# Two of four weight block sums of a Strassen product made by accumulating DMAs

## The chip, the cores and the metric

The kernel runs on one core of one Trainium2 chip. The metric is the device time of one execution in microseconds; before and after the change it is the median of several runs.

## The reference

One layer of a hybrid diffusion backbone is computed for 128 context tokens and 512 latent tokens (640 in all, width 1024) with shared weights in float32:

```
u = RMSNorm(h) * (1 + scale1) + shift1
z = u @ w_in                       # 1024 x 6656, split into q, k, v, B, C, x_in, g_att, g_conv
A = GQA attention(q, k, v) @ w_att_out
Bm = (B * dwconv3(C * x_in)) @ w_conv_out
h = h + gate1 * RMSNorm((sigmoid(g_att) * A + sigmoid(g_conv) * Bm) @ w_o)
h = h + gate2 * RMSNorm(conv_ffn(RMSNorm(h) * (1 + scale2) + shift2))
```

The change touches the product `u @ w_in` for the columns of g_att, C, x_in, B and g_conv.

## The kernel before

Every float32 operand of a product is split into a high part (a cast to float32r on ScalarE, `hi_of`, L1174) and a low part (the rest, a subtraction on VectorE, `lo_of`, L1178). A product is then three matmuls: high x high, high x low and low x high. Right operands (the tokens' side) are kept in that form for the whole stage; weights come through the sync engine (SP) into a pool of three rooms `raw` of 128 x 1024 and are split on the way.

The columns of `w_in` named above are worked through in 19 pairs of blocks of 128 columns (`PAIRS`: three for g_att, then C, X, B for each of four indices, then four for g_conv). Each pair is one step of Strassen's algorithm in Winograd's form: the weights of a pair are four blocks, each 512 deep and 128 wide. They are a11 and a12, the upper and the lower half in depth of the first column block, and a21 and a22 of the second one. Seven products of 12 matmuls (128 x 128 x 320) are made instead of eight, in the order A11, A12, S2, S1, S3, S4, A22. `PLACE` says in which part and half the left operand of each lies. Four of them are sums of blocks, kept in `MS`, four parts of 512 columns in `WB`: M1 = a21 + a22 (step S1), M2 = M1 + a11 (S2), M3 = a11 + a21 (S3) and M4 = M2 + a12 (S4). They are all additions; the signs are in the right operands and in the results.

`mix(m)` issues pair m. TensorE, ScalarE and VectorE run in the order in which the code is written (`manual_schedule`); between two steps stand the copies out of PSUM (`copied`, `added`), the splits for later steps (`mhi` for ScalarE's half, `lo_of` for VectorE's), the sums of the next pair (`msums`, three groups of additions at L1282), and extra work that comes with the results of the pair before (`more`: gates, convolution taps, shift sums `shift_add` in `XG`). Part 0 of the left operands is a11 and a12, part 1 is M1 and M2, part 2 is M3 and M4, part 3 is a22.

The sync engine's and GpSimd's queues are ordered by a scheduler in this stage; each of them runs its entries in turn, and an entry that waits holds the later ones. `mload(n)` loads a whole column block (512 KB) into the next room of the pool: `mix` calls it for the two blocks of the pair after next. After the last pair the same function loads `w_conv_out` in blocks for the next stage. Outside the stage GpSimd does attention work (L879) and norms; within it, it has nothing.

Of the kernel before, what the change touches and what calls it, by code (L numbers as in the profile page):

```python
# [14 lines left out]
ALU = mybir.AluOpType  # L15
# [3 lines left out]
KT = 8  # L19
# [44 lines left out]
def trunk_layer(ctx, tc, x_prompt, x_sample, cache_k, cache_v, c, c_ctx, w_ada, b_ada, g_pre1, g_post1, g_pre2,  # L64
                g_post2, w_in, q_norm, k_norm, w_att_out, conv_w, w_conv_out, w_o, w_up, conv_ffn, w_down, rope,
                y_prompt, y_sample, new_k, new_v):
    nc = tc.nc
    V, S, G, PE = nc.vector, nc.scalar, nc.gpsimd, nc.tensor

    w_ada, b_ada, w_in, w_o, w_up, w_down = w_ada[0], b_ada[0], w_in[0], w_o[0], w_up[0], w_down[0]  # L70
    w_att_out, w_conv_out, conv_w, conv_ffn = w_att_out[0], w_conv_out[0], conv_w[0], conv_ffn[0]
# [22 lines left out]
    def nm(s):  # L94
        cnt[0] += 1
        return f"{s}_{cnt[0]}"
# [19 lines left out]
    def ps2():  # L116
        return ps.tile([128, 1024], F32, tag="s2", name=nm("s2"), bufs=3)

    def ps1():
        return psa.tile([128, 512], F32, tag="s1", name=nm("s1"), bufs=2)  # L120
# [9 lines left out]
    def raw_tile():  # L130
        return wp.tile([128, 1024], F32, tag="raw", name=nm("raw"), bufs=3)
# [192 lines left out]
    with tc.tile_pool(name="pro", bufs=2) as pro, tc.manual_schedule(engines={mybir.EngineType.SP}):  # L324
# [237 lines left out]
        for f in range(2, KT):  # L562
# [5 lines left out]
            if f == 2:  # L568
# [11 lines left out]
                both = [kvp_.tile([128, 9, HD], F32, name=x) for x in ("tabq", "tabk")]  # L580
# [24 lines left out]
            if f == KT - 2:  # L605
                cut_upto(9)
                p = ps1()
# [16 lines left out]
    with tc.tile_pool(name="att", bufs=2) as at:  # L624
# [329 lines left out]
        p = ps2()[:, 0:512]  # L954
# [205 lines left out]
    def bank(i):  # L1160
        if i >= 2 and len(pools) == 1:
            early.close()
            pools.append(ctx.enter_context(tc.tile_pool(name="pb", bufs=1, space=bass.MemoryType.PSUM)))
        return pools[i >= 2].tile([128, 512], F32, tag=f"b{i}", name=nm(f"b{i}"))


    cut, raws, pair, TT = {}, {}, {}, {}

    def hi_of(key, raw, to=None):
        n = raw.shape[1]  # L1170
        if to is None:
            to = tuple(wp.tile([128, 1024], F32R, tag=x, name=nm(x), bufs=3)[:, :n] for x in ("whi", "wlo"))
        cut[key] = (raw, *to)
        S.activation(to[0], raw, AF.Copy)  # L1174

    def lo_of(key):
        raw, hi, lo = cut[key]
        V.tensor_tensor(out=lo, in0=raw, in1=hi.bitcast(F32), op=ALU.subtract)  # L1178

    def block(out, key, half, right, start, stop):  # L1180
        _, hi, lo = cut[key]
        wh, wl = (y[:, half * 512:half * 512 + 512] for y in (hi, lo))
        th, tl = TT[right]
        for k in range(4):
            ws = slice(k * 128, (k + 1) * 128)
            for n, (p, q) in enumerate(((wh, th), (wh, tl), (wl, th))):
                PE.matmul(out, p[:, ws], q[:, k, :], start=start and k == 0 and n == 0, stop=stop and k == 3 and n == 2,  # L1187
                          skip_group_check=True)
# [28 lines left out]
    MS = WB[:, 2 * NTOK:2 * NTOK + 2048]  # L1217
# [37 lines left out]
    PAIRS = [("GA", i) for i in range(1, 4)] + [(x, i) for i in range(4) for x in "CXB"] + [("GC", i) for i in range(4)]  # L1255
    NP = len(PAIRS)
    AT = {"GA": O_GA, "C": O_C, "X": O_X, "B": O_B, "GC": O_GC}
    ROWS_OF = {"C": 0, "X": 1, "B": 2}

    def mrows(m):  # L1260
        x, i = PAIRS[m]
        r = ROWS_OF[x] if x in ROWS_OF else (i - 1 if x == "GA" else i)
        return ROWS[2 * r], ROWS[2 * r + 1]

    def col_load(key, w, c0):
        raw = raws[key] = raw_tile()
        nc.sync.dma_start(raw.rearrange("p (k c) -> p k c", c=128), w[:, c0:c0 + 128].rearrange("(k p) c -> p k c", p=128))

    def mload(n):

        if n < 2 * NP:
            x, i = PAIRS[n // 2]
            col_load(("m", n // 2, n % 2), w_in, AT[x] + (2 * i + n % 2) * 128)
        elif n < 2 * NP + KT:
            col_load(("v", n - 2 * NP), w_conv_out, (n - 2 * NP) * 128)

    def msums(m):
        a1, a2 = raws["m", m, 0], raws["m", m, 1]
        s1, s2, s3, s4 = (MS[:, i * 512:(i + 1) * 512] for i in range(4))

        def add(out, a, b):
            V.tensor_tensor(out=out, in0=a, in1=b, op=ALU.add)  # L1282

        def both():
            add(s1, a2[:, 0:512], a2[:, 512:1024])
            add(s3, a1[:, 0:512], a2[:, 0:512])
        return both, lambda: add(s2, s1, a1[:, 0:512]), lambda: add(s4, s2, a1[:, 512:1024])

    def mhi(m, part):
        src = {0: raws["m", m, 0], 1: MS[:, 0:1024], 2: MS[:, 1024:2048], 3: raws["m", m, 1][:, 512:1024]}[part]  # L1290
        hi_of(("m", m, part), src)

    def vcut(j):
# [3 lines left out]
    def mix(m, extra):  # L1297

        d0, d1 = mrows(m)
        nxt = m + 1 if m + 1 < NP else None  # L1300
        pair["m", m] = tuple(bank((3 * m + i) % 8)[:, 0:HT] for i in range(3))

        def step(x):
            b = 1 if x == "A12" else 2 if x in ("S1", "S4") else 0
            part, half = PLACE[x]
            block(pair["m", m][b], ("m", m, part), half, "m" + RIGHT[x], x in ("A11", "A12", "S1"), True)

        def more(i):
            for f in extra.get(i, ()):
                f()  # L1310

        if m:
            mix_last(m - 1)
        lo_of(("m", m, 1))
        more(0)
        step("A11")

        copied(("m", m), "p1", 0, HT)
        more(1)
        step("A12")  # L1320

        mhi(m, 2)
        added(d0[:, 0:HT], ("m", m), "p1", 1)
        lo_of(("m", m, 2))
        more(2)
        step("S2")

        copied(("m", m), "u2", 0, HT)
        more(3)
        step("S1")  # L1330

        copied(("m", m), "p5", 2, HT)
        mhi(m, 3)
        adds = msums(nxt) if nxt else None
        if nxt:
            adds[0]()
        more(4)
        step("S3")

        added(d1[:, HT:], ("m", m), "p5", 0)  # L1340
        lo_of(("m", m, 3))
        mload(2 * m + 4)
        if nxt:
            mhi(nxt, 0)
            lo_of(("m", nxt, 0))
            adds[1]()
        else:
            vcut(0)
        more(5)
        step("S4")  # L1350

        if nxt:
            mhi(nxt, 1)
        added(d0[:, HT:], ("m", m), "u2", 2)
        if nxt:
            adds[2]()
        mload(2 * m + 5)
        more(6)
        step("A22")

    def mix_last(m):
        S.activation(mrows(m)[1][:, 0:HT], pair["m", m][0], AF.Copy)
# [8 lines left out]
    for j in range(KT):  # L1371
        unit = next_unit()
        if j == 6:
            for n in range(3):
                mload(n)
        if j < 6:
            for f in making[2 * j:2 * j + 2]:
                f()
        elif j == 7:
            adds = msums(0)  # L1380
            adds[0]()
            mhi(0, 0)
            lo_of(("m", 0, 0))
            adds[1]()
            mhi(0, 1)
            adds[2]()
            mload(3)
        outs = plain_gemm(j, *unit.parts, AH, AL)
        for out, (b0, b1) in zip(outs, BLKS):
            if j < 2:  # L1390
                times(MA[:, j, b0:b1], out, MA[:, KT - 2 + j, b0:b1])
            else:
                S.activation(MA[:, j, b0:b1], out, AF.Copy)
# [53 lines left out]
    for m, (x, i) in enumerate(PAIRS):  # L1447
# [18 lines left out]
        elif before[0] == "X":  # L1466
            c0, c1, y0, y1 = ROWS[:4]
# [7 lines left out]
        elif before[0] == "B":  # L1475
            c0, c1, y0, y1, b0, b1 = ROWS[:6]
# [28 lines left out]
    for j in range(KT):  # L1505
        if j + 1 < KT:
            vcut(j + 1)
        else:
            cut_upto(state["next"] + 1)
        if 0 < j < KT - 3:  # L1510
            mload(2 * NP + j + 3)
        elif j:
            fetch(state["next"] + min(j - 4, 2))
        if j == 0:
            gate_load(graws[0], 2, 0)
        if j < KT - 1:
            gate_load(graws[j + 1], 2, j + 1)
        if j == 5:
            gate_vectors(gvec, 2, g_post1)
        _, hi, lo = cut["v", j]  # L1520
        outs = plain_gemm(j + 2, hi, lo, BH, BL)
        sg = ROWS[j]
        for h, (out, (b0, b1)) in enumerate(zip(outs, BLKS)):
            times(sg[:, b0:b1], out, sg[:, b0:b1])
            if h == 0 and j:
                gate_add(gaccs, graws[j], j, 0)
        V.tensor_tensor(out=sg, in0=sg, in1=MA[:, j, :], op=ALU.add)
        for row in range(0 if j == 0 else 1, 2):
            gate_add(gaccs, graws[j], j, row)
        mh, ml = MH[j // 4][:, j % 4, :], ML[j // 4][:, j % 4, :]  # L1530
        S.activation(mh, sg, AF.Copy)
        minus(ml, sg, mh.bitcast(F32))
# [389 lines left out]
    for q in range(4):  # L1922
# [7 lines left out]
        elif q == 1:  # L1930
            half_load(0)
            p = bank(6)
# [114 lines left out]
    adds = right_sums(0, HALF)  # L2047
# [18 lines left out]
    adds = sums(2)  # L2066
# [103 lines left out]
    w, x, y = NJ - 3, NJ - 2, NJ - 1  # L2170
# [96 lines left out]
```

## Time and profile before

| what | us |
|---|---|
| median of 3 runs | 1110.13 (1109.88 to 1110.19) |
| span of the profiled execution | 1108.4 |
| stage of the 19 pairs, about | 320 to 555 |
| TensorE busy in the span | 1098.6 |
| VectorE busy | 843.6 |
| ScalarE busy | 577.2 |
| GpSimd busy | 145.4 |

The span runs from the first to the last instruction of the profiled execution; it is 1.7 us below the median of the runs, and the profile states no other time for that execution. In the profile's lines, PE is TensorE's matmul, PEld its weight load (which overlaps PE), DVE is VectorE, ACT ScalarE, POOL GpSimd, SPq the queue of the sync engine. A line `L1282 DVE ... x18 | 12.3, 686 | 1.1 <-DMA raw` reads: line of the code, engine, operation, tiles, count, busy microseconds in total, mean nanoseconds of one, idle microseconds just before, and what ended them. In an order of time the first number is the start, the second the length.

### The profile page before, as it was taken

How to read it: one execution, taken by the hardware profiler on the slowest of the kernel's cores; microseconds unless marked ns; L12 is line 12 of the kernel's file. 1: busy time of each engine (PE TensorE's matmuls, PEld its weight loads, DVE VectorE, ACT ScalarE, POOL GpSimd, SP SyncE). 2: the span in 40 equal slices, each digit the busy share in tenths (PEclk: the TensorE clock that was granted, in tenths of full speed). 3: DMA queues.
4: the chain of work that ended last, by engine and by line, in shares of the span. 5: the costliest groups of instructions: out<-in, count | busy, mean ns of one | idle time of the engine just before them, and what ended most of it. 6: DMA issues, size and time to landing. Idle time of an engine off the chain costs nothing.

```text
span 1108.4 us, 19227 instructions
## 1 busy us (share of the span) xinstructions
PE 1098.6 (99%) x7633; PEld 1012.9 (91%) x7633; DVE 843.6 (76%) x1352; ACT 577.2 (52%) x1021; POOL 145.4 (13%) x190
## 2 busy tenths in 40 slices
PE   8999999999999999999999999999999999999998
PEld 6798888889999999999999789999999999998886
DVE  5687766755559889988678558898899889989544
ACT  5486776764335444455422356655565545546442
POOL 1067666651000000000000021000000000000001
PEclk9999999999999999999999999999999999999999
DMA  9832102102224323332254655234344333435722
GB/s 318 246 101 79 58 25 73 39 4 73 76 78 130 108 79 99 108 89 77 81 188 151 212 170 153 77 101 126 112 133 132 106 114 119 127 101 184 261 93 95
DMA packets 157415, 130.07 MB, mean 117 GB/s; under 512 B 6410, under 2 KB 135942, under 8 KB 157326
## 3 DMA queue, kind: packets, MB, share of 16 engines
q1 hardware_dynamic: 157214, 128.81, 37.9%
q8 instruction: 60, 0.98, 0.4%
q14 instruction: 29, 0.24, 0.1%
q10 hardware_dynamic: 112, 0.04, 0.0%
HBM read 117.39 MB, written 11.44 MB: 116 GB/s over the span
## 4 chain that ended last, share of the span: by engine, by line
PE 97%; DMA 2%; ACT 1%; DVE 0%; issue 0%; DVEq 0%; SPq 0%; ACTq 0%
PE b L1187 46%; PE b L183 10%; PE b L185 10%; PE b L184 9%; PE s L704 3%; PE s L892 3%; PE s L183 3%; PE s L916 3%; PE s L185 3%; PE s L184 3%; DMA raw<-in_w_in_dram 1%; DMA araw<-in_w_ada_dram 1%; PE b L1786 1%; PE s L675 0%; PE s L238 0%; DMA XT<-in_x_sample_dram 0%
## 5 line engine op out<-in xcount | busy, mean ns | idle before, releaser
L1187 PE MATMUL b<-ZBr,whi 128*128 128x320 f32 x688 | 152.1, 309 | 0.0
L1187 PE MATMUL b<-MT,whi 128*128 128x320 f32 x608 | 134.2, 309 | 0.0
L1187 PEld LDWEIGHTS b<-ZBr,whi 128*128 128x128 f32 x688 | 115.0, 188 | 0.1
L1187 PE MATMUL b<-ZBr,wlo 128*128 128x320 f32 x344 | 106.2, 309 | 0.0
L1187 PEld LDWEIGHTS b<-MT,whi 128*128 128x128 f32 x608 | 101.6, 188 | 0.0
L1187 PE MATMUL b<-MT,wlo 128*128 128x320 f32 x304 | 94.1, 309 | 0.0
L879 POOL TENSOR_TENSOR pr<-pr,sm 128x640 f32<-128x640 f32 x64 | 80.0, 1260 | 53.7 <-DVE sm L878 47.4
L1174 ACT ACTIVATE whi<-SUM 128x1024 fp32r<-128x1024 f32 x40 | 42.2, 1055 | 78.5 <-DVE SUM L1701 76.0
L1731 DVE SCALAR_TENSOR_TENSOR Y<-C,cffn,Y 128x642 f32<-128x642 f32 x88 | 77.6, 882 | 0.9
L149 DVE TENSOR_TENSOR wlo<-raw,whi 128x1024 fp32r<-128x1024 f32 (+1 forms) x32 | 35.4, 1106 | 54.9 <-ACT whi L148 54.6
L869 ACT ACTIVATE pr<-s,mx,rq 128x640 f32<-128x640 f32 x64 | 56.6, 885 | 32.5 <-DVE mx L856 29.1
L1187 PE MATMUL b<-ZBT,whi 128*128 128x320 f32 x320 | 71.1, 309 | 0.0
L1187 PE MATMUL b<-UL,whi 128*128 128x320 f32 x228 | 70.8, 311 | 0.0
L1187 PE MATMUL b<-UH,wlo 128*128 128x320 f32 x228 | 70.1, 307 | 0.0
L1187 PE MATMUL b<-UH,whi 128*128 128x320 f32 x228 | 69.7, 306 | 0.0
L1174 ACT ACTIVATE whi<-WB 128x1024 fp32r<-128x1024 f32 x38 | 40.1, 1055 | 55.8 <-DVE WB L1282 55.8
L1178 DVE TENSOR_TENSOR wlo<-raw,whi 128x1024 fp32r<-128x1024 f32 (+1 forms) x51 | 50.4, 1018 | 20.1 <-ACT whi L1174 20.1
L1187 PEld LDWEIGHTS b<-ZBr,wlo 128*128 128x128 f32 x344 | 64.6, 188 | 0.0
L183 PE MATMUL s<-whi,UH 128*128 128x256 f32 (+1 forms) x197 | 64.4, 327 | 0.0
L851 DVE TENSOR_REDUCE mx<-s 128x1 f32<-128x640 f32 x64 | 52.5, 820 | 14.0 <-PE s L704 13.5
L1195 ACT ACTIVATE p<-b 128x320 f32<-128x320 f32 x78 | 34.1, 438 | 55.3 <-PE b L1187 53.5
L185 PE MATMUL s<-whi,UL 128*128 128x256 f32 (+1 forms) x197 | 59.9, 304 | 0.0
(401 smaller groups left out, 3191.7 us busy)
## 6 DMA issues: line engine op xcount, KB each, us to landing
raw<-in_w_in_dram SPq DMA_DIRECT2D x48, 512.0 KB
RAW<-in_w_up_dram SPq DMA_DIRECT2D x40, 512.0 KB
raw<-in_w_down_dram SPq DMA_DIRECT2D x22, 512.0 KB
raw<-in_w_ada_dram SPq DMA_DIRECT2D x16, 512.0 KB
actd<-Y SPq DMA_DIRECT2D x18, 321.0 KB
XT<-in_w_ada_dram SPq DMA_DIRECT2D x9, 512.0 KB
raw<-in_w_att_out_dram SPq DMA_DIRECT2D x8, 512.0 KB
raw<-in_w_conv_out_dram SPq DMA_DIRECT2D x8, 512.0 KB
```

The source lines that it names most:

```text
L149: V.tensor_tensor(out=lo[:, :n], in0=raw, in1=hi[:, :n].bitcast(F32), op=ALU.subtract)
L183: PE.matmul(out, ah, bh, start=start, stop=False)
L184: PE.matmul(out, ah, bl, start=False, stop=False)
L185: PE.matmul(out, al, bh, start=False, stop=stop)
L851: V.tensor_reduce(out=mx, in_=self.sc[h], axis=AX.X, op=ALU.max, negate=True)
L869: S.activation(pr, self.sc[h], AF.Exp, bias=mx, scale=rs, accum_out=sm)
L879: G.tensor_tensor(out=pr, in0=pr, in1=sm.broadcast_to((128, NTOK)), op=ALU.mult)
L1174: S.activation(to[0], raw, AF.Copy)
L1178: V.tensor_tensor(out=lo, in0=raw, in1=hi.bitcast(F32), op=ALU.subtract)
L1187: PE.matmul(out, p[:, ws], q[:, k, :], start=start and k == 0 and n == 0, stop=stop and k == 3 and n == 2, skip_group_check=True)
L1195: S.activation(t, pair[j][b], AF.Copy)
L1731: V.scalar_tensor_tensor(out=y, in0=crows(j)[i][:, d:d + NACT], scalar=cffn[:, 44 * d + o:44 * d + o + 1], in1=y, op0=ALU.mult, op1=ALU.add)
```

## The change

Of each pair's blocks, the two sums M1 and M3 are no longer added by VectorE. The sync engine loads block a21 into the place of the sum, once for M1 and once for M3, and GpSimd issues a transfer from SBUF to SBUF that adds a22 (for M1) or a11 (for M3) to what lies there. The first column block (a11 and a12) has two rooms in turn, a22 two halves of a third room; these three rooms of the pool stay with the stage for its length. VectorE keeps the two other additions, M2 and M4. The loads are issued at other points of `mix`: into M1 after its low part has been made, into M3 likewise, a1 (a11 and a12) of the pair after next before step S3, a22 after it.

```diff
--- before.py
+++ after.py
@@ -1266,28 +1266,43 @@
         raw = raws[key] = raw_tile()
         nc.sync.dma_start(raw.rearrange("p (k c) -> p k c", c=128), w[:, c0:c0 + 128].rearrange("(k p) c -> p k c", p=128))
 
-    def mload(n):
-
-        if n < 2 * NP:
-            x, i = PAIRS[n // 2]
-            col_load(("m", n // 2, n % 2), w_in, AT[x] + (2 * i + n % 2) * 128)
-        elif n < 2 * NP + KT:
-            col_load(("v", n - 2 * NP), w_conv_out, (n - 2 * NP) * 128)
+    M1, M2, M3, M4 = (MS[:, i * 512:(i + 1) * 512] for i in range(4))
+    mrooms = {}
+
+    def mrooms_open():
+        a, b, c = (raw_tile() for _ in range(3))
+        mrooms["a1"], mrooms["a22"] = (a, b), (c[:, 0:512], c[:, 512:1024])
+
+    def mload(m, what):
+
+        if m >= NP:
+            j = 2 * (m - NP) + (what == "a22")
+            if what in ("a1", "a22") and j < KT:
+                col_load(("v", j), w_conv_out, j * 128)
+            return
+        x, i = PAIRS[m]
+        row, k, nk = {"a1": (0, 0, 8), "a22": (1, 4, 4), "s1": (1, 0, 4), "s3": (1, 0, 4)}[what]
+        if what in mrooms:
+            dst = raws["m", m, what] = mrooms[what][m % 2]
+        else:
+            dst = {"s1": M1, "s3": M3}[what]
+        c0 = AT[x] + (2 * i + row) * 128
+        nc.sync.dma_start(dst.rearrange("p (k c) -> p k c", c=128),
+                          w_in[k * 128:(k + nk) * 128, c0:c0 + 128].rearrange("(k p) c -> p k c", p=128))
+        if what == "s1":
+            G.dma_start(dst, raws["m", m, "a22"], accum_op=ALU.add)
+        elif what == "s3":
+            G.dma_start(dst, raws["m", m, "a1"][:, 0:512], accum_op=ALU.add)
 
     def msums(m):
-        a1, a2 = raws["m", m, 0], raws["m", m, 1]
-        s1, s2, s3, s4 = (MS[:, i * 512:(i + 1) * 512] for i in range(4))
+        a1 = raws["m", m, "a1"]
 
         def add(out, a, b):
             V.tensor_tensor(out=out, in0=a, in1=b, op=ALU.add)
-
-        def both():
-            add(s1, a2[:, 0:512], a2[:, 512:1024])
-            add(s3, a1[:, 0:512], a2[:, 0:512])
-        return both, lambda: add(s2, s1, a1[:, 0:512]), lambda: add(s4, s2, a1[:, 512:1024])
+        return lambda: add(M2, M1, a1[:, 0:512]), lambda: add(M4, M2, a1[:, 512:1024])
 
     def mhi(m, part):
-        src = {0: raws["m", m, 0], 1: MS[:, 0:1024], 2: MS[:, 1024:2048], 3: raws["m", m, 1][:, 512:1024]}[part]
+        src = {0: raws.get(("m", m, "a1")), 1: MS[:, 0:1024], 2: MS[:, 1024:2048], 3: raws["m", m, "a22"]}[part]
         hi_of(("m", m, part), src)
 
     def vcut(j):
@@ -1312,6 +1327,8 @@
         if m:
             mix_last(m - 1)
         lo_of(("m", m, 1))
+        if nxt:
+            mload(nxt, "s1")
         more(0)
         step("A11")
 
@@ -1322,6 +1339,8 @@
         mhi(m, 2)
         added(d0[:, 0:HT], ("m", m), "p1", 1)
         lo_of(("m", m, 2))
+        if nxt:
+            mload(nxt, "s3")
         more(2)
         step("S2")
 
@@ -1332,18 +1351,17 @@
         copied(("m", m), "p5", 2, HT)
         mhi(m, 3)
         adds = msums(nxt) if nxt else None
-        if nxt:
-            adds[0]()
+        mload(m + 2, "a1")
         more(4)
         step("S3")
 
         added(d1[:, HT:], ("m", m), "p5", 0)
         lo_of(("m", m, 3))
-        mload(2 * m + 4)
+        mload(m + 2, "a22")
         if nxt:
             mhi(nxt, 0)
             lo_of(("m", nxt, 0))
-            adds[1]()
+            adds[0]()
         else:
             vcut(0)
         more(5)
@@ -1353,8 +1371,7 @@
             mhi(nxt, 1)
         added(d0[:, HT:], ("m", m), "u2", 2)
         if nxt:
-            adds[2]()
-        mload(2 * m + 5)
+            adds[1]()
         more(6)
         step("A22")
 
@@ -1371,20 +1388,19 @@
     for j in range(KT):
         unit = next_unit()
         if j == 6:
-            for n in range(3):
-                mload(n)
+            mrooms_open()
+            for m, what in ((0, "a1"), (0, "a22"), (0, "s1"), (0, "s3"), (1, "a1"), (1, "a22")):
+                mload(m, what)
         if j < 6:
             for f in making[2 * j:2 * j + 2]:
                 f()
         elif j == 7:
             adds = msums(0)
-            adds[0]()
             mhi(0, 0)
             lo_of(("m", 0, 0))
+            adds[0]()
+            mhi(0, 1)
             adds[1]()
-            mhi(0, 1)
-            adds[2]()
-            mload(3)
         outs = plain_gemm(j, *unit.parts, AH, AL)
         for out, (b0, b1) in zip(outs, BLKS):
             if j < 2:
@@ -1508,7 +1524,7 @@
         else:
             cut_upto(state["next"] + 1)
         if 0 < j < KT - 3:
-            mload(2 * NP + j + 3)
+            mload(NP + (j + 3) // 2, ("a1", "a22")[(j + 3) % 2])
         elif j:
             fetch(state["next"] + min(j - 4, 2))
         if j == 0:
```

## The prediction

> **What bounds the kernel now.** I read the page first, then the windows of the stage that the change touches (the 19 pairs of column blocks, 320 to 555 us), TensorE's waits in it, the groups of instructions by shape, and last the order of time on VectorE for single pairs.
>
> ```profile
> span 1108.4 us, 19227 instructions
> ...
> PE 1098.6 (99%) x7633; PEld 1012.9 (91%) x7633; DVE 843.6 (76%) x1352; ACT 577.2 (52%) x1021; POOL 145.4 (13%) x190
> ...
> L879 POOL TENSOR_TENSOR pr<-pr,sm 128x640 f32<-128x640 f32 x64 | 80.0, 1260 | 53.7 <-DVE sm L878 47.4
> ```
> ```profile
> core 0: us, PE busy (x) PEld busy (x) DVE busy (x) ACT busy (x) POOL busy (x), PEclk, DMA share, GB/s
> 320.00:555.00 235.00, 235.00 (x1611) 233.78 (x1610) 196.90 (x283) 115.50 (x181) 0.00 (x0) 1.00 0.34 97
> ```
> ```profile
> PEld b L1187 <- issue: 0.6, 1, 0.6
> PEld b L1441 <- issue: 0.2, 1, 0.2
> PEld b L301 <- issue: 0.2, 1, 0.2
> PEld b L1187 <- DVE wlo L1178: 0.2, 1, 0.2
> ```
>
> TensorE sets the end: 99% busy over the whole span, busy all through the stage at a granted clock of 1.00. All the gaps before its weight loads in the stage add up to 1.2 us, and only 0.2 us of them ended with VectorE. VectorE is busy 196.9 of 235 us there, GpSimd not at all, and the DMA engines 34%. So work that is taken off VectorE has almost nothing to give back; what matters is whether the new route delivers in time.
>
> ```profile
> 320.18 135.05 PE b L1187 x924
> ```
>
> 924 matmuls are 11 pairs of 84, so a pair takes 12.28 us and a step (12 matmuls) 1.75 us. Pair m starts at 320.18 + 12.28 m; its third step, S2, 3.5 us later.
>
> **What is removed.** Per pair two additions on VectorE go: a21+a22 (S1's block, M1) and a11+a21 (S3's block, M3).
>
> ```profile
> L1282 DVE TENSOR_TENSOR WB<-raw 128x512 f32<-128x512 f32 x18 | 12.3, 686 | 1.1 <-DMA raw<-in_w_in_dram 0.9
> L1282 DVE TENSOR_TENSOR WB<-raw,raw 128x512 f32<-128x512 f32 x18 | 12.3, 684 | 0.0
> ```
>
> That is 12.3 + 12.3 = 24.6 us of VectorE in this window. All of it lies beside matmuls, so it is worth at most the 0.2 us that TensorE waited for VectorE, and nothing more.
>
> **What is added, and how it is chained.** For each pair the sync engine now loads a21 twice, into M1 and into M3 (256 KB each), and GpSimd adds a22 and a11 to these with an accumulating transfer of 256 KB, which must wait until the plain load has landed. In the order in which the changed kernel issues its transfers, the queue of the sync engine runs per pair: a1 of the pair after next, s1 (into M1), s3 (into M3), a22. GpSimd's queue holds only the two accumulations in turn. Two of the waits are new and tie these queues into one chain: a1 goes into a room from which the last s3 accumulation still reads, so it waits for that to land; and s1, which stands behind a1 in the queue, waits with it. VectorE then waits for M1 before its first remaining addition, with everything behind it (the other addition, the copies out of PSUM, the low part for S1 and S2).
>
> Where VectorE frees M1 and M3 is seen in pair 2 (start 344.74):
>
> ```profile
> 345.40 1.23 DVE L1178 TENSOR_TENSOR wlo<-WB,whi 128x1024 fp32r<-128x1024 f32 x1 [0.21 <-ACT whi L1174]
> 346.54 1.94 DVE L292 SCALAR_TENSOR_TENSOR XG<-XG,s 128x768 f32<-128x768 f32 x2
> ...
> 349.21 1.23 DVE L1178 TENSOR_TENSOR wlo<-WB,whi 128x1024 fp32r<-128x1024 f32 x1 [0.32 <-ACT whi L1174]
> 350.35 1.55 DVE L1366 TENSOR_TENSOR MA<-MA,WA 128x640 f32<-128x640 f32 x2
> ...
> 355.76 0.68 DVE L1282 TENSOR_TENSOR WB<-WB,raw 128x512 f32<-128x512 f32 x1
> ...
> 357.65 1.23 DVE L1178 TENSOR_TENSOR wlo<-WB,whi 128x1024 fp32r<-128x1024 f32 x1 [0.21 <-ACT whi L1174]
> ```
>
> The first row is the low part of M1 and M2: from its end, 346.54, s1 may be loaded. The third is the low part of M3 and M4: from 350.35, 3.81 us later, s3 may be loaded. The addition at 355.76 is the first that needs the new M1; from its start to the end of the next pair's low part (357.65 + 1.14, the spacing of the first two rows) are 3.03 us. That end, 358.8, is 1.7 us ahead of pair 3's S2 (357.02 + 3.5 = 360.5): TensorE's margin.
>
> The step from the one low part to the other differs by pair:
>
> ```profile
> 373.25 1.22 DVE L1178 TENSOR_TENSOR wlo<-WB,whi 128x1024 fp32r<-128x1024 f32 x1
> ...
> 383.48 1.55 DVE L1366 TENSOR_TENSOR WA<-WA 128x640 f32<-128x640 f32 x2
> ...
> 388.59 1.00 DVE L1406 SCALAR_TENSOR_TENSOR WA<-WA,feat 128x127 f32<-128x127 f32 x2
> ...
> 395.88 1.01 DVE L1406 SCALAR_TENSOR_TENSOR WA<-WA,feat 128x127 f32<-128x127 f32 x2
> ...
> 400.52 1.55 DVE L1201 TENSOR_TENSOR BL<-WA,BHa 128x640 fp32r<-128x640 f32 x2
> ```
>
> Four pairs with a shift addition as above 3.81; four after an X pair 5.11 (383.48 to 388.59); four after a B pair 4.64 (395.88 to 400.52); the other five of 17 about 1.6, where only a copy (0.40) and this 1.22 stand between. Mean: (4 x 3.81 + 4 x 5.11 + 4 x 4.64 + 5 x 1.6) / 17 = 3.66 us.
>
> What a transfer takes, from the shift weights, the one load of this stage for which VectorE is seen to wait right after its issue:
>
> ```profile
> 447.11 0.34 SPq L276 DMA_DIRECT2D XG<-in_w_ada_dram  x1
> ...
> 450.34 1.95 DVE L292 SCALAR_TENSOR_TENSOR XG<-XG,s 128x768 f32<-128x768 f32 x2 [0.53 <-DMA XG<-in_w_ada_dram]
> ...
> DMA packets 144, 0.39 MB, mean 197 GB/s; under 512 B 16, under 2 KB 16, under 8 KB 144
> ```
>
> The third row is the DMA view of the 2.0 us in which another such load moved. Issue to use is 3.23 us; 0.39 MB at 197 GB/s is 1.98, so 1.25 us are fixed. A plain 256 KB (0.262 MB) then takes 1.33 + 1.25 = 2.6 us, and s1 behind a1 (0.786 MB) 4.0 + 1.25 = 5.25.
>
> No row shows an accumulating transfer, A from here on. Lower bound: 2.6 us, a plain one; below that it cannot be, since it moves no less. Upper bound: both operands fetched as whole transfers one after the other, GpSimd's share as large as its nearest operation (L879, 1.26 us), and a 512 KB load ahead of it: 1.26 + 2 x 2.6 + 2.6 = 9.1. I take 1.26 for GpSimd, 1.25 fixed, 2 x 1.33 for two operands, and half of a 256 KB load that shares the engines (0.67), since s3 or a22 is on its way then: A = 5.84 us, an estimate from these rows.
>
> One rule speaks for less. The Trainium skill, "DMA: Bandwidth & Descriptors" (section on the anatomy of a DMA of the GpSimd path), fits such a transfer with 2.0 us plus the bytes at 436 GB/s, which by that page would be 2.6 us for 256 KB; the sum would then come out hidden. No run here shows it, and the fit is not for an accumulation.
>
> **The sum.** From the low part of one pair to that of the pair after next: 3.66 (to M3's release) + 2.6 (s3) + A + 5.25 (a1, s1) + A + 3.03 (addition, cast, low part) = 14.54 + 2A. Two pairs of TensorE are 24.56, so it is hidden up to A = 5.0. With 5.84 the two pairs take 26.2, a pair 13.1: 0.83 us over 12.28. Over 17 pairs 14.0 us. By the lower bound nothing is added, by the upper (32.7 per two pairs) 4.1 x 17 = 69 us.
>
> The rest costs nothing. The first pair: s1 and s3 may load when T4 is made.
>
> ```profile
> 304.45 1.49 DVE L1238 TENSOR_TENSOR MT<-WB,MT 128x1280 fp32r<-128x1280 f32 x1 [1.35 <-ACT MT L1237]
> ...
> 315.73 1.41 DVE L1282 TENSOR_TENSOR WB<-WB,raw 128x512 f32<-128x512 f32 x2
> ```
>
> That is 305.9; both loads (0.52 MB) land by 309.9, the accumulation by 315.7, when its reader stood before. With A = 9.1 the low part would be late by 3.2 us, and S2 starts only at 323.7, so TensorE is still covered. The shift loads behind s1 wait for additions that VectorE does after M1's low part anyway. w_conv_out's first blocks take the rooms as these come free, in the same places of the queue. The extra traffic (256 KB of loads and two accumulations per pair) raises the 34% without filling the engines.
>
> The sum stands on the span of 1108.4 us; the median of the runs, 1110.1, is 1.7 above it, and I add to the median: 1110.1 + 14.0 = **1124 us**. About 0.2% (2.2 us) is what a measurement of this kernel can tell from no change.
>
> **Rivals.** First, hidden: A is at most 5.0 us, and the two waits end before TensorE needs them. For it: 1.7 us of margin, an idle GpSimd, free DMA engines. Against: the chain passes through two accumulations in two pairs, so every microsecond of A counts twice. Time: 1110.1 less the 0.2 us gap, 1109.9. I give it 0.30, and it is the case that ends on the other side of mine: it decides at A = 5.0.
>
> Second, faster by over 0.2%: VectorE, relieved by 1.37 us per pair, no longer delays TensorE anywhere. Against: even all gaps of the stage are 1.2 us, so 1108.9 at the best, which is within 0.2%; it would need waiting that the modelled ends of matmuls hide. 0.03.
>
> Third, GpSimd gets its descriptors out late because VectorE holds what they share. VectorE is busy 84% of the stage; if each accumulation had to sit out one stretch such as that from 345.40 to 348.48 (3.1 us without a pause), A is 8.9, a pair 16.2 and the time 1110.1 + 3.9 x 17 = 1176. No row of the stage has GpSimd at work, so nothing speaks for it but that share. The Trainium skill, "SBUF — State Buffer" (who interferes with whom), has such starvation only for VectorE's two-port modes, which it denies to instructions on two tensors, as most of these are; by that page it would hardly happen here, and no run so far shows it. 0.07, out of the 0.67 for slower.
>
> **How the numbers follow.** Slower than by 0.2%: 0.67, within: 0.30, faster: 0.03. My value of A lies 0.8 us above the point of decision, between 2.6 and 9.1. The range must take in the hidden case, so it starts at 1109.3; upwards I go to A = 7.7 (a pair 14.97, 2.7 x 17 = 45 us), 1155. The slower case's own range is 1113 to 1155.
>
> **What would show it.** Right: in the trace after, VectorE waits for a DMA into WB ahead of the addition M1 + a1 in most pairs, TensorE's weight loads wait for the low part of WB, 12 to 24 matmuls into a pair, pairs stand 13 us apart, and an accumulation takes 5 to 7 us from the landing of its plain load. Wrong: 12.3 us between pairs and no DMA wait on VectorE (A under 5.0); or TensorE's new gaps end with something other than WB; or a1 does not wait for the accumulation, which breaks the chain.

## The result, and the profile after

The changed kernel takes 1113.95 us (median of 5 runs, 1113.67 to 1115.62), the kernel before 1110.19 beside it (1109.88 to 1110.61): ratio 1.0037, 95% interval 1.0026 to 1.0048. It is slower, as forecast, but by 3.8 us and not by 14. The profiled execution has a span of 1113.8 us (1108.4 before); it is the slowest of the five runs (1115.62 us), so it shows some 1.7 us more of loss than the median.

The page of the kernel after, its busy times and the queue of GpSimd's transfers:

```profile
span 1113.8 us, 19460 instructions
...
PE 1100.9 (99%) x7633; PEld 1014.8 (91%) x7633; DVE 822.2 (74%) x1314; ACT 577.4 (52%) x1021; POOL 179.2 (16%) x228
...
q0 software_dynamic: 5472, 9.96, 5.4%
```

The windows of the stage after: the whole, and three stretches. The columns are the window, its length, the busy times of TensorE (matmuls, weight loads), VectorE, ScalarE and GpSimd, the granted clock, the DMA share and GB/s.

```profile
321.00:558.00 237.00, 233.92 (x1595) 231.48 (x1594) 175.17 (x246) 115.30 (x180) 31.17 (x36) 1.00 0.63 153
366.70:390.40 23.70, 23.07 (x159) 22.81 (x158) 18.75 (x27) 10.95 (x19) 3.46 (x4) 1.00 0.67 161
409.60:428.90 19.30, 18.24 (x123) 17.57 (x122) 13.92 (x21) 9.94 (x16) 2.62 (x3) 1.00 0.63 158
428.90:461.20 32.30, 30.91 (x211) 29.61 (x211) 25.36 (x36) 12.49 (x20) 4.33 (x5) 1.00 0.68 160
```

VectorE lost 22 us of its work and the DMA engines went from 0.34 to 0.63 busy. All that TensorE idles in the 237 us (237.00 - 233.92 = 3.08) lies in the three stretches: 0.63 + 1.06 + 1.39. From the first matmul of each pair to that of the next (every 84th matmul of L1187 in the trace), less the 12.28 us of a pair, five pairs and the sum over all 19 are, for the kernels without a delay put in (labels as in the experiments, one profiled execution each; 0.0 stands for a pair up to 0.03 under 12.28):

```
us over 12.28          pair 5  pair 8  pair 9  pair 10  pair 11   all 19
before                   0.17    0.0     0.0     0.85     0.10      1.24
after                    0.88    1.72    0.0     2.72     0.08      5.55
no accumulation          0.06    0.06    0.0     1.07     0.08      1.41
plain GpSimd transfer    0.68    0.38    0.0     2.58     0.10      3.88
queue in program order   0.26    2.00    0.0     1.02     0.86      4.99
M1 accumulated alone     1.00    1.47    0.16    1.58     0.26      5.50
M3 accumulated alone     0.76    0.77    0.30    2.56     0.40      6.29
shift sum moved          0.76    1.50    0.38    0.85     0.76      4.47
```

The change lost 5.55 - 1.24 = 4.3 us, 0.7 in pair 5, 1.7 in pair 8, 1.9 in pair 10, and nothing in the other sixteen. That is more than the 3.08 of idle time: the rest stands in the view as busy matmuls, whose ends the profile models. The spans differ by 5.4; 0.9 of that lies ahead of the stage, which starts later here. What VectorE waited for, in the view of waits from 300 to 560 us, agrees. It waited for a DMA into the sums (WB) only three times, 2.6 us in all:

```profile
DVE XG L292 <- DMA XG<-in_w_ada_dram: 3.8, 1, 3.8
DVE WB L1301 <- DMA WB<-raw: 2.6, 3, 1.6
```

**Pair 5** shows the predicted chain at work. The chain of waits after, from 355 to 386 us, long pieces, and with it GpSimd's order of time and VectorE's:

```profile
366.79 0.50 DVE WA L1198
...
367.56 4.89 DMA WB<-raw
...
372.52 0.37 SPq L1290
...
373.00 4.37 DMA WB<-in_w_in_dram
...
377.92 4.07 DMA WB<-raw
...
382.02 0.70 DVE WB L1301
```
```profile
367.56 0.86 POOL L1295 DMA_DIRECT2D WB<-raw  x1 [1.03 <-DVE WA L1198]
```
```profile
358.61 1.23 DVE L1178 TENSOR_TENSOR wlo<-WB,whi 128x1024 fp32r<-128x1024 f32 x1 [0.25 <-ACT whi L1174]
359.75 1.94 DVE L292 SCALAR_TENSOR_TENSOR XG<-XG,s 128x768 f32<-128x768 f32 x2
...
362.38 1.23 DVE L1178 TENSOR_TENSOR wlo<-WB,whi 128x1024 fp32r<-128x1024 f32 x1 [0.28 <-ACT whi L1174]
363.52 1.55 DVE L1383 TENSOR_TENSOR MA<-MA,WB 128x640 f32<-128x640 f32 x2
...
382.02 0.69 DVE L1301 TENSOR_TENSOR WB<-WB,raw 128x512 f32<-128x512 f32 x1 [0.75 <-DMA WB<-raw]
...
385.11 1.55 DVE L1383 TENSOR_TENSOR WA<-WA 128x640 f32<-128x640 f32 x2
...
389.08 1.21 DVE L1178 TENSOR_TENSOR wlo<-WB,whi 128x1024 fp32r<-128x1024 f32 x1
```

Read from the top of VectorE's rows: pair 3's low part of M1 and M2 ends at 359.75, that of M3 and M4 at 363.52; M3's accumulation starts at 367.56 and lands at 372.45; a1 was held in the sync engine's queue until then and s1 behind it; M1's accumulation starts at 377.92 and lands at 381.99, where VectorE has stood for 0.75 us; pair 5's low part ends at 385.11. That low part is in time for S2. But all that VectorE does behind it is 0.75 us later, and the low part for S3 had no room. VectorE's order of time before:

```profile
387.45 1.21 DVE L1178 TENSOR_TENSOR wlo<-WB,whi 128x1024 fp32r<-128x1024 f32 x1
```

VectorE's next instruction started at 388.59, and S3 was due at 320.18 + 5 x 12.28 + 4 x 1.75 = 388.6. After, this low part starts at 389.08, 1.6 us later; 0.9 of that is the later start of the stage, and 0.7 is the wait.

**Pair 8** comes out at TensorE in the same way, after a wait of 1.59 us (420.52, L1301), but another step of the chain was long there. The chain of waits after, from 408 to 432 us:

```profile
410.47 5.69 DMA WB<-in_w_in_dram
...
416.78 3.72 DMA WB<-raw
```

M3's accumulation, started at 405.65, took 4.2 us and landed at 409.86, and a1 left the queue at 410.00. The accumulation into M1 took 3.72 us, less than in pair 5. But s1's load behind a1 took 5.69 us from its issue, where it took 4.37 in pair 5: from the landing into M3 to the start of M1's accumulation 6.9 us passed. Why this load was slower is open.

**Pair 10** is another matter: its shift weights. In VectorE's order of time after:

```profile
455.75 1.95 DVE L292 SCALAR_TENSOR_TENSOR XG<-XG,s 128x768 f32<-128x768 f32 x2 [3.75 <-DMA XG<-in_w_ada_dram]
```

In the chain of waits that load is

```profile
450.49 5.16 DMA XG<-in_w_ada_dram
```

It took 3.2 us before. a1 and s1 now stand directly ahead of it in the queue; s1 is issued at 449.36.

**A itself**, from the instructions of GpSimd on WB after (durations in ns: least, median, most):

```profile
L1293 POOL DMA_DIRECT2D WB<-raw x19: 865/865/1087, 310.4 to 541.7; - x19
L1295 POOL DMA_DIRECT2D WB<-raw x19: 865/865/1199, 311.3 to 544.7; - x19
...
DMA to landing us min/median/max: 3.3/3.8/5.1
```

A is 3.8 us and not 5.84, and GpSimd's own part of it 0.865 us with least and median alike.

### The profile page after: what moved, and what is told of

The parts are those of the page before. It is cut to its first block, busy times and chain, and to the rows that moved or that the text cites. A ratio compares the mean times of both kernels' runs of the same rounds, so it can differ in the third digit from the quotient of the medians.

```text
span 1113.8 us, 19460 instructions
## 1 busy us (share of the span) xinstructions
PE 1100.9 (99%) x7633; PEld 1014.8 (91%) x7633; DVE 822.2 (74%) x1314; ACT 577.4 (52%) x1021; POOL 179.2 (16%) x228
## 4 chain that ended last, share of the span: by engine, by line
PE 91%; DMA 4%; DVE 2%; ACT 1%; issue 1%; SPq 0%; DVEq 0%; POOL 0%; ACTq 0%; POOLq 0%
PE b L1187 40%; PE b L183 9%; PE b L185 9%; PE b L184 9%; PE s L704 3%; PE s L892 3%; PE s L183 3%; PE s L916 3%; PE s L185 3%; PE s L184 3%; DMA WB<-raw 1%; DMA WB<-in_w_in_dram 1%; DVE wlo L1178 1%; PE s L414 1%; DMA XT<-in_x_sample_dram 1%
## 5 line engine op out<-in xcount | busy, mean ns | idle before, releaser
L1187 PE MATMUL b<-ZBr,whi 128*128 128x320 f32 x688 | 152.1, 309 | 0.0
L1187 PE MATMUL b<-MT,whi 128*128 128x320 f32 x608 | 134.5, 309 | 1.5 <-DVE WA L1198 1.4
L1187 PEld LDWEIGHTS b<-ZBr,whi 128*128 128x128 f32 x688 | 114.9, 188 | 0.1
L1187 PE MATMUL b<-ZBr,wlo 128*128 128x320 f32 x344 | 106.1, 309 | 0.0
L1187 PEld LDWEIGHTS b<-MT,whi 128*128 128x128 f32 x608 | 101.5, 188 | 2.0 <-issue 1.6
L1187 PE MATMUL b<-MT,wlo 128*128 128x320 f32 x304 | 94.3, 310 | 1.6 <-DVE wlo L1178 1.6
L1187 PE MATMUL b<-ZBT,whi 128*128 128x320 f32 x320 | 71.1, 309 | 0.0
L1187 PE MATMUL b<-UL,whi 128*128 128x320 f32 x228 | 70.8, 311 | 0.0
L1187 PE MATMUL b<-UH,wlo 128*128 128x320 f32 x228 | 70.1, 307 | 0.0
L1187 PE MATMUL b<-UH,whi 128*128 128x320 f32 x228 | 69.7, 306 | 0.0
L1187 PEld LDWEIGHTS b<-ZBr,wlo 128*128 128x128 f32 x344 | 64.6, 188 | 0.0
```

## The experiments

The theory after the result: the accumulations make the loss, through waits in single pairs and a crowded queue; A, the time from the start of an accumulation to its landing, is too short to hold up the whole stage. The rivals: the second load of a21 and the traffic alone; a1's place in the queue; VectorE's order.

**Without the accumulations.** Both transfers of GpSimd are left out, and so two of the four sums; the loads stay.

```diff
-            G.dma_start(dst, raws["m", m, "a22"], accum_op=ALU.add)
+            pass
...
-            G.dma_start(dst, raws["m", m, "a1"][:, 0:512], accum_op=ALU.add)
+            pass
```

> Both accumulating transfers are left out (M1 and M3 hold a21 alone, so the sums lack a22 and a11 and the output is not the reference's); the loads, their number and their places stay. Theory: with no accumulation in the chain all waits go, also that for the shift weights in pair 10, and the time is that of before, 1110.0 to 1110.5. If a wait in pair 10 of over 2 us stays, it is due to the added and later loads and not to the accumulations: then about 1112.

1111.37 us, ratio 1.0009 (1.0000 to 1.0018). TensorE's pieces in the chain of waits from 318 to 562 us:

```profile
320.46 135.24 PE b L1187 x924
456.48 36.95 PE b L1187 x252
493.60 61.54 PE b L1187 x420
```

924 matmuls run through, as before, and the stage loses 0.2 us in this execution. By the medians the loads cost 1.0 us of the 3.8, with an interval from 0 to 2.0; the accumulations make the rest, by their waits, their traffic or both.

**A plain transfer in their place.** GpSimd copies where it added (the sums are left out).

```diff
-            G.dma_start(dst, raws["m", m, "a22"], accum_op=ALU.add)
+            G.dma_start(dst, raws["m", m, "a22"])
...
```

> The two GpSimd transfers per pair copy a22 and a11 over M1 and M3 instead of adding to them, so the sums are left out; every transfer, wait and byte that is written stays. If the adding itself is what makes an accumulation long, the landing falls from 3.3/3.8/5.1 us (least, median, most) to about the 2.6 us of a plain 256 KB load, the waits of VectorE for WB (2.6 us in three) go, pairs 5 and 8 lose their 0.7 and 1.7 us, and the time is about 1111.5. If a transfer of GpSimd from SBUF to SBUF takes that long whether it adds or not, the landing stays within 0.2 us of 3.8 and the time at 1113.9 within 0.5.

1112.62 us, ratio 1.0020 (1.0011 to 1.0029). GpSimd's instructions on WB:

```profile
L1293 POOL DMA_DIRECT2D WB<-raw x19: 548/548/780, 310.2 to 539.4; - x19
...
DMA to landing us min/median/max: 2.2/2.8/4.4
```

So adding costs 1.0 us of landing, 0.32 of it on GpSimd, and pair 8 loses most of its gap (1.72 to 0.38); pair 5 hardly, pair 10 not. In pair 5 the plain transfer into M1 is itself the longest, 4.43 us from its start at 376.83. The landing comes out near the first expectation, the time between the two.

**The queue in the order of the program** (s1, s3, a1, a22, so that a1 no longer stands ahead of s1).

```diff
+    inorder.enter_context(tc.manual_schedule(engines={mybir.EngineType.SP}))
```

> The changed kernel with one difference: in the stage of the pairs the sync engine's queue runs in the order in which the code is written, so that a1 of the pair after next is issued behind s1 and s3, at a place where the accumulation that reads its room has long landed. Theory (the queue order chains s1 to the s3 accumulation through a1): VectorE's waits for the accumulation into M1 (0.75 and 1.59 us in pairs 4 and 7) go, TensorE's gaps of 0.8 and 1.6 us in pairs 5 and 8 go with them, and the time falls by about 2.4 us to some 1111.5; the wait of 3.75 us for the shift weights in pair 10 may shrink too, since a1 no longer stands right before them, and then 1110. Rival (the accumulations' traffic slows every load): waits and time stay, 1113 to 1114. Rival (an accumulation is too slow by itself, whatever stands before it): the same.

1113.92 us, ratio 1.0027 (1.0016 to 1.0037). Pairs 5 and 10 lose most of their new gaps, pair 8 keeps its own, and pairs 11 and 12 have new ones (0.86 and 0.45). In VectorE's order of time, and among GpSimd's instructions of L1293:

```profile
419.31 0.69 DVE L1301 TENSOR_TENSOR WB<-WB,raw 128x512 f32<-128x512 f32 x1 [1.87 <-DMA WB<-raw]
```
```profile
DMA to landing us min/median/max: 3.3/4.5/7.2
```

The wait moved rather than went: a1's 512 KB are now issued close to M1's accumulation, which lands up to 7.2 us after its start. In pair 8 a1 goes out at 412.10, a load of shift weights and M1's accumulation at 413.54; in pair 11, the one with 7.2 us, a1 goes out 0.1 us behind the accumulation. So a1's place explains pair 5 of the kernel after, and in pair 8 other traffic is enough for a wait.

**One sum alone by accumulation** (first M1, then M3), the other added by VectorE in place.

```diff
-            G.dma_start(dst, raws["m", m, "a1"][:, 0:512], accum_op=ALU.add)
+            pass
...
+            add(M3, M3, a1[:, 0:512])
```
```diff
-            G.dma_start(dst, raws["m", m, "a22"], accum_op=ALU.add)
+            pass
...
+            add(M1, M1, raws["m", m, "a22"])
```

> Only M1 is made by an accumulating transfer; M3 is loaded with a21 by the sync engine as in the changed kernel, but a11 is added by VectorE in place, just before M2 (0.68 us more of VectorE per pair). No accumulation reads a1 any more, so a1 waits for none. Theory: no wait for the accumulation into M1 is left in pairs 4 and 7, 1110 to 1111.5, with VectorE's wait in pair 10 deciding. Rival (traffic): half of the accumulations' traffic is left, so half of the loss, about 1112. Rival (the M1 accumulation is too slow by itself): the waits stay, 1113 to 1114.

> Only M3 is made by an accumulating transfer; M1 is loaded with a21 and a22 is added by VectorE in place, before M2 (0.68 us more of VectorE per pair). a1 still waits for the s3 accumulation, and s1 behind it, but after s1 only the plain load is left. Theory: one accumulation (3.8 us) less in the chain; VectorE waits nowhere in pairs 4 and 7; only the 0.75 and 1.59 us are gained back and the wait in pair 10 may stay: 1110.5 to 1112. Rival (traffic): about 1112, with the wait in pair 10 halved. Rival (M1's accumulation too slow by itself): like the theory, so this run tells only traffic apart.

1114.88 us (1.0042, 1.0030 to 1.0055) and 1115.65 (1.0047, 1.0034 to 1.0060). VectorE waits for an accumulation 1.0 us in two, and never. Neither is faster than with two accumulations, and the intervals overlap. The addition that came back stands later in VectorE's order than it did before, in front of M2's addition and the next low part; that this eats the gain is likely and not tested. The two runs do not tell the accumulations apart.

**VectorE's order.** The taps of the convolution moved one slot later, the shift sum of pair 10 moved to pair 9, both, and both on the kernel before.

```diff
-            also(1, conv_tap, y0, c0, e, 0)
+            also(2, conv_tap, y0, c0, e, 0)
...
-    SHIFTS = {(0, 4): 0, ..., (7, 4): 5, (10, 1): 6, (10, 4): 7}
+    SHIFTS = {(0, 4): 0, ..., (7, 4): 5, (9, 4): 6, (10, 4): 7}
```

> The changed kernel, with two convolution taps (L1422, 1.9 us of VectorE in each of the four pairs that follow an X pair) moved from before the low part of M3 and M4 to behind it. Theory (in these pairs VectorE reaches that low part with no time to spare before step S3, so any wait for the accumulation one pair earlier comes out at TensorE in full): the waits of 0.75 and 1.59 us in pairs 4 and 7 stay, the gaps of TensorE in pairs 5 and 8 (0.7 and 1.7 us over before) go, the gap of pair 10 stays: 1111.5. Rival (the accumulations slow VectorE or the loads in general): the gaps move to other pairs, 1113 to 1114.

> The changed kernel, with the seventh of the eight shift additions moved from the start of pair 10 to the middle of pair 9, so that the load of the last shift weights has most of a pair in place of 3 us. Theory: VectorE's wait of 3.75 us for these weights goes and with it the 1.9 us of pair 10; the gaps of pairs 5 and 8 stay: 1112. Rival (general slowing): 1113 to 1114.

> The changed kernel with both moves, the taps behind the low part and the shift addition into pair 9. Theory: no gap of the stage is left that before does not have, 1110 or a little less (before itself loses 0.2 us in pair 5 and some in pair 10). Rival (general slowing): 1112 or more.

> The kernel before with the same two moves, as the control for the run of the changed kernel with both. Theory: before has only 0.2 us of gap in pair 5 and 0.4 us in pair 10 beyond the gate sums, so it gains 0.2 to 0.6 us: 1109.6 to 1110.2, not to be told from before. If it gains over 1 us, the moves do more than make room for the accumulations.

1115.16 (1.0041, 1.0026 to 1.0055), 1113.90 (1.0030, 1.0018 to 1.0041), 1114.62 (1.0036, 1.0023 to 1.0049) and, on the kernel before, 1116.56 (1.0055, 1.0041 to 1.0068). With the shift sum moved, no wait for XG is left and pair 10 is at its 0.85 of before, so the late shift weights are the cause there; but pairs 9 and 11 lose 0.4 and 0.7 in turn. The control shows that the two moves together cost 6 us without the change: VectorE's order has no room for this work at these places. The expectations that the taps would give time back were wrong.

**A made longer.** GpSimd multiplies M1 and M3 by 1 in place ahead of the accumulation, once, twice and four times; then half of the columns; then M1 alone and M3 alone; then once with the queue in the order of the program.

```diff
+        if what in ("s1", "s3"):
+            for _ in range(1):
+                G.tensor_scalar(out=dst, in0=dst, scalar1=1.0, scalar2=None, op0=ALU.mult)
```

> GpSimd multiplies M1 and M3 by 1 in place (128 x 512) between the landing of the plain load and the accumulation, which lengthens A by one such operation, some 1 us, to about 4.8 us. The sum of the prediction (14.54 + 2A) gives 24.1 us for two pairs, still under 24.56: no loss from the chain as a whole, and only the single pairs that already wait lose more, 1 us each in pairs 5 and 8: about 1116. The rival, that the chain has slack that the sum does not see and only the waits in single pairs count once, gives the same here; a chain shorter on slack than the sum gives 1120 or more.

> Two such operations, A about 5.8 us, the value of the prediction. By its sum the two pairs take 26.1 to 26.2 us, a pair 13.1, and the time is 1110.3 + 14 = 1124. If the delay is felt once in each pair after an X pair and nowhere else, it is 1110.3 + 3.8 + 2 x 4 = about 1122, with the other pairs at 12.28; the two are told apart by the distances of the pairs, 13.1 in all or 14 in four. The order of two shift loads in the queue of the sync engine differs a little from the kernel after.

> Four such operations, A about 7.8 us. By the sum of the prediction two pairs take 30.1 us, a pair 15.07, and the time is 1110.3 + 2.79 x 17 = 1158. If the chain is not tied as the sum has it (each pair's delay felt once, against its own slack of 1 to 2 us), it is at most 2 us in each pair, 1110.3 + 34 = 1144 or less.

> Both accumulations wait for an operation on half of the columns (256 of 512), about 0.8 us and 0.3 of idle time: A about 4.8 us. If the loss begins at A = 5.0, as the prediction's sum has it, the time is 1114 to 1116, with single pairs late as in the kernel after. If it begins near 4.0 (33 us over 17 pairs is 1.9 us a pair at A = 5.9), it is 1110.3 + 0.8 x 17 = about 1124.

> Only M1 is multiplied by 1 by GpSimd ahead of its accumulation, which gives that one about 2.2 us more (1.94 for the operation and 0.3 of idle time in the run with one operation on both). By the predicted chain, which holds one accumulation of M1 and one of M3 in two pairs, this is half of the delay on both: about 1110.3 + 16 = 1126. If the single room of M1 carries the loss, it is all of it: 1138 to 1143.

> Only M3 is delayed, by the same 2.2 us. By the predicted chain half of the loss of both again, about 1126. If the single room of M1 carries it, hardly anything: 1114 to 1117.

> One operation on both, as in the run that took 1143, with the queue of the sync engine in the order of the program (s1, s3, a1, a22), in which a1 no longer stands ahead of s1. By the predicted chain, which this takes apart, most of the loss goes: 1115 to 1120. If the single room of M1 carries it, 1138 or more stays.

GpSimd's groups from 300 to 592 us (count, busy us, mean ns, idle before), one fence each for the run with one operation, with half of one, with M1 alone and M3 alone:

```profile
L1294 POOL TENSOR_SCALAR WB<-WB 128x512 f32<-128x512 f32 x38 | 72.5, 1909 | 204.7 <-DMA WB<-in_w_in_dram 186.0 <-DVE WA L1198 8.1 <-DVE XG L292 7.5
L1298 POOL DMA_DIRECT2D WB<-raw x19 | 17.5, 920 | 5.3 <-POOL WB L1294 5.3
```
```profile
L1294 POOL TENSOR_SCALAR WB<-WB 128x256 f32<-128x256 f32 x38 | 45.4, 1195 | 220.5 <-DMA WB<-in_w_in_dram 188.4 <-DVE BL L1201 14.7 <-DVE WA L1198 8.9
```
```profile
L1294 POOL TENSOR_SCALAR WB<-WB 128x512 f32<-128x512 f32 x19 | 33.8, 1777 | 223.5 <-DMA WB<-in_w_in_dram 196.5 <-DVE WA L1425 17.9 <-DVE MA L1386 9.0
```
```profile
L1294 POOL TENSOR_SCALAR WB<-WB 128x512 f32<-128x512 f32 x19 | 35.9, 1892 | 22.4 <-DMA WB<-in_w_in_dram 20.3 <-DVE wlo L1178 1.1 <-DVE WB L1198 0.9
```

An operation took 1.91 us and not the 1 expected, and 5.3 / 19 = 0.28 us passed between it and the accumulation. So A grew by 2.19 us with one operation and by 1.48 with half of one: to 5.99 and 5.28 if the landing is left at 3.8, and to 5.8 and 5.4 with the medians of these runs, 3.6 and 3.9. The table has the first.

```
kernel                     us       ratio (95%)                 A     over before
plain GpSimd transfer    1112.62   1.0020 (1.0011 to 1.0029)   2.8       2.3
after                    1113.95   1.0037 (1.0026 to 1.0048)   3.8       3.8
half an operation        1131.59   1.0188 (1.0173 to 1.0204)   5.3      21.3
one operation            1143.14   1.0291 (1.0275 to 1.0307)   6.0      32.8
M1 alone                 1133.07   1.0201 (1.0185 to 1.0217)             22.7
M3 alone                 1125.94   1.0141 (1.0126 to 1.0156)             15.6
one, program order       1134.24   1.0211 (1.0194 to 1.0228)             23.9
two operations           1181.31   1.0638 (1.0619 to 1.0657)             71.0
four operations          1291.29   1.1626 (1.1610 to 1.1642)            181.0
```

From half to one, 0.71 us of A cost 11.5 us, 16 us for each, near the 17 of the prediction's sum (once in each of 17 pairs); with the medians of the two runs it is 0.4 us of A and 28 for each. So the slope is not measured well. Drawn back along 17, the loss starts at 5.28 - 21.3/17 = 4.03 and at 5.99 - 32.8/17 = 4.06; with the medians and one slope or the other, it starts at 3.9 to 4.6. So the **point of decision is A = 4.0 us by estimate**, with 3.9 to 4.6 by these other readings, where the prediction had 5.0. The run with half an operation took the side of 4.0 (1124 expected there, 1116 for 5.0), and more.

Two and four operations were expected at 1124 and 1158, with 1 us for each. In these runs GpSimd's queue did M3's before M1's accumulation in many pairs (in order of time, four in a row, here with two on each):

```profile
390.65 6.56 POOL L1294 TENSOR_SCALAR WB<-WB 128x512 f32<-128x512 f32 x4 [7.65 <-DMA WB<-in_w_in_dram]
```

so their A is not a clean one, and they say only that it goes on. The granted clock fell as well: over 320 to 587 us it was 0.99 with half an operation and 0.98 with one, over 320 to 650 us 0.94 with two and 0.81 with four. A part of these losses is therefore clock, by estimate at most 0.02 x 267 = 5 us with one operation and 0.19 x 330 = 63 with four.

M1 alone and M3 alone cost 22.7 and 15.6: neither all nor nothing. M3's is what the predicted chain gives; so the rival by which M1's single room carries all of it falls. But M1 costs more than its half (the landings of its run were longer too, at the median 4.3 us against 3.5 with M3 alone), and in the order of the program, which takes a1 out of the chain, 23.9 of 32.8 us stay, against my 5 to 10. The chain of waits of that run shows why:

```profile
364.03 2.81 DMA WB<-in_w_in_dram
...
367.02 1.73 POOL WB L1294
...
369.04 4.82 DMA WB<-raw
...
373.88 0.70 DVE WB L1304
...
374.73 1.07 ACT whi L1174
...
375.83 1.24 DVE wlo L1178
...
377.08 2.92 DMA WB<-in_w_in_dram
```

From s1's load to s1's next load, 13.05 us, in one pair of 12.28: load, operation, accumulation, addition, cast, low part, and M1 has one room. This second chain was not in the prediction. It too closes once in each pair, so the slope of the delayed kernels does not tell the two chains apart. With A = 3.8 and no operation it needs, by estimate, 2.8 + 0.2 + 3.8 + 3.2 = 10 us and stays hidden, unless the accumulation stretches as it does in pair 8 of the run in program order.

## Why the prediction was right or wrong

Right: the sign; that TensorE gains nothing from VectorE's relief; and the chain (M3's accumulation holds a1, a1 holds s1), which the rows of pairs 3 to 5 show step by step. The slope of 17 us for 1 us of A is neither confirmed nor refuted. What failed was the sum: its term A was put 2 us too high (5.84 for 3.8), its other term 1.9 too low (14.54 for 16.40 in pairs 3 to 5), and a mean was taken for all pairs. With both terms as measured the sum is 16.4 + 2 x 3.8 = 24.0 of 24.56 and forecasts no loss, so the sign was in part luck: the loss came from three single pairs, one of them by a wait that I had priced at nothing.

**The term A** was 5.84 and measured 3.8. GpSimd's share is 0.865 us and not 1.26, and the rest 2.9 and not 4.58: I had priced two operands as two transfers one after the other and added half of a load. A plain transfer lands in 2.8 us, near the lower bound of 2.6, and adding costs 1.0 more. The Trainium skill, "DMA: Bandwidth & Descriptors" (anatomy of a DMA of the GpSimd path), has a fit of 2.0 us plus the bytes at 436 GB/s, by estimate 2.6 us here; the trace agrees for the plain transfer (least 2.2, median 2.8), not for the accumulation.

**The term 14.54** was too short. In the rows of pairs 3 to 5 it is 385.11 - 359.75 - 4.89 - 4.07 = 16.40, in a pair of the kind that I put at 3.81 and so at 14.69. The step from the low part of M3 and M4 to the start of its accumulation is 4.04 us instead of the 2.6 of the load. GpSimd stands idle for the last 1.03 of it, which the view puts down to L1198 on VectorE; I had priced no such wait, and how much of the 1.03 is still the load the view does not say. The other steps fit (3.77 for 3.81, 5.47 for 5.25, 3.12 for 3.03). With 16.40 the point of decision is (24.56 - 16.40) / 2 = 4.08. That is near the 4.0 of the delayed kernels, but it is worked out from this one pair; in pair 8 the step of 5.47 took 6.9.

**The mean** was the step that decided the answer. At A = 3.8 against 4.0 the chain is hidden on average, which is the first rival, with 1109.9 us; the time is 4 us above that. A mean over 17 pairs hides that pairs 5 and 8 take longer, and what they lose, 2.4 us, no later pair gives back. On the way to pair 5 the two accumulations were 4.89 and 4.07 us, not 3.8: with them the two pairs need 25.36 of 24.56. On the way to pair 8 they were 4.2 and 3.7, and it was a1 and s1 that took 6.9 us in place of 5.25. And I took TensorE's margin from S2 of pair 3 (1.7 us), where a delay of 0.75 does not show; in pairs 5 and 8 the low part for S3 had none.

**"The shift loads behind s1 wait for additions that VectorE does after M1's low part anyway"**, priced at nothing, was worth 1.9 us: the order of the queue changed around them, and the load of pair 10 came 3.75 us too late for VectorE.

The signs that I named as showing it wrong came: pairs of 12.28 us for the most part, waits for WB in three pairs and not in most. The third rival, GpSimd starved, has no trace in its 865 ns; the Trainium skill, "SBUF — State Buffer" (who interferes with whom), has copies of VectorE stall such a transfer and additions of two tensors not. On the additions the trace agrees, with 865 ns at the least and at the median; it has no copy of VectorE beside a transfer to try the other half.

Open stays why M3's accumulation waits for VectorE at all, why the plain transfer into M1 took 4.43 us in pair 5, and how the loss divides between the accumulations' waits and their traffic: no run keeps the one without the other. None of the variants beats the kernel before.

## What to carry to other kernels

A sum moved to a transfer is free only while load, transfer and reader fit between the time its room comes free and the time it is read, so write down every chain that closes on a room or on a queue, with the period it must fit, and check the worst pair and the consumer with the least margin, not the mean and the first consumer. Where TensorE was the bound, taking 22 us off VectorE earned nothing, and a changed order of a queue delayed a load whose wait had been priced at nothing. A delay put into the disputed step brackets the point at which a chain begins to bind, if the delay, the landings and the granted clock are measured in the same run.

## What was not expected of the hardware

An accumulating transfer of 256 KB in SBUF costs GpSimd 865 ns where a plain one costs 548, lands in 3.8 us where the plain one needs 2.8, and its queue from 325 to 540 us, in the DMA view after and then with plain transfers, shows a difference of the same sense (packets, MB, share of the 16 engines):

```profile
q0 software_dynamic: 4896, 8.92, 25.2%
```
```profile
q0 software_dynamic: 2665, 8.69, 10.9%
```

Nearly the same bytes go in 1.8 times the packets and take 2.3 times the time of the engines. Its landing is no constant either: 3.3 us at the least, up to 7.2 in the order of the program, where a 512 KB load was issued 0.1 us behind it. And the same multiplication of 128 x 512 took GpSimd between 1.48 and 2.59 us in the run with one operation; what stretched it was not tried.
